# The first feed-forward product of a transformer block, with 20 of its 22 gated pairs as 7 block products in place of 8

## The chip, the cores and the metric

The kernel runs on one core of a Trainium2 chip. The metric is the time of one execution on the device in microseconds (us), as the median of several runs; lower is better. A core has five engines with a queue of instructions each: TensorE (PE, matrix products), VectorE (DVE), ScalarE (ACT), GpSimd (POOL) and SyncE (SP, which here issues loads). Each engine works through its own queue in order; semaphores make it wait for the others. Products accumulate in PSUM; all other data lies in SBUF, 128 partitions wide.

## The reference

One block over 512 latent tokens and 256 context tokens with 1024 features, in fp32. Its last part is what is changed here:

```
def _swiglu(u, w_in, w_out):
    a, b = jnp.split(u @ w_in, 2, axis=-1)
    return (jax.nn.silu(a) * b) @ w_out
...
        x = x + g2 * _swiglu(_modulate(_rms_norm(x, norm2_g[i]), sh2, sc2),
                             w_ffn_in[i], w_ffn_out[i])
```

`u` is 512 x 1024, `w_in` 1024 x 5632, `w_out` 2816 x 1024. The parts ahead (two token mixers and their projections) are the same in both kernels.

## The kernel before

Features lie on the partitions, tokens in the columns. An fp32 operand is split into a rounded part `hi` (type fp32r) and the rest `lo` (`split`, lines 217 to 219: a cast on ACT, a subtraction on DVE). A product of two such operands is three matmuls, `mm3`, lines 245 to 248: hi by hi, hi by lo, lo by hi.

The 2816 hidden features are 22 tiles of 128. Tile j needs a pair of weight tiles, one for `a` (through SiLU) and one for `b`. Each weight tile is 128x1024 (8 steps of 128 input features by 128 outputs) and comes by one load of 512 KB on SP into a ring of three buffers (`wraw`, NRAW = 3); its hi and lo parts lie in rings of four (`whi`, `wlo`). `blk` gives larger buffers from a common pool; a buffer there is free again when its last reader is done.

Pairs 0 and 1 are special: their weights (`wff`) are loaded early, and they are multiplied for the tokens 0 to 255 (A) and then 256 to 511 (B), in a section whose order is written out by hand (`tc.manual_schedule`, for PE, DVE and ACT). The norm of the tokens (`mod2`) is done there too, by the same halves, into `u2` (hi and lo for each of 8 feature tiles). For pairs 2 to 21, outside that section, a planner that lays the program out against its own estimate of the times sets the order of the instructions on each engine. A pair there is two `mm_tile` calls of 24 matmuls with 512 columns, each into a PSUM bank (`ps_f`), then `swiglu`: SiLU on ACT, a multiplication by the second tile on DVE, and the split of the result `h` into hi and lo. The next stage, `ffn_out`, multiplies the 22 h tiles by `w_out` (`wfo`), into `ps_fo`.

Of the kernel before, what the change touches and what calls it, by code (L numbers as in the profile page):

```python
# [56 lines left out]
# column map of the packed per-feature vectors  # L57
# [15 lines left out]
def block_kernel(ctx: ExitStack, tc: tile.TileContext, a, out):  # L73
# [90 lines left out]
    silc = cst.tile([P, NK, 4], F32, name="silc")  # silu(c), silu(c_ctx), 0, 0  # L164
# [9 lines left out]
    def rsqrt(v, n, nm):  # L174
        """v (fp32 [P, n]) -> 1/sqrt(v), Newton from an integer seed."""
# [10 lines left out]
    def sumsq_step(acc, ap, k, eng=vec):  # L186
        """acc += ap ** 2 (features on partitions)"""
        sq = tmp("sq")[:, :ap.shape[1]] if k else acc
        act.activation(sq, ap, AF.Square)
        if k:  # L190
            eng.tensor_tensor(acc, acc, sq, op=ALU.add)

    def part_sum(*parts):
        """-1/(2 D) * sum over the partitions, on every partition"""
        ps = psx("st")[:, :parts[0].shape[1]]
        for i, t in enumerate(parts):
            pe.matmul(ps, lhsT=halfd, rhs=t, start=i == 0, stop=i == len(parts) - 1)
        return ps
# [4 lines left out]
    def inv_newton(y, ps):  # L203
        """y = (1.5 + (ps - EPS / 2) * y * y) * y"""
# [5 lines left out]
    def inv_rms(ps):  # L210
        """1 / sqrt(mean square + EPS)"""
# [39 lines left out]
    s4 = cst.tile([P, NK, 2, 2], F32, name="s4")      # [feature tile, (shift, scale), (x, ctx)]  # L251
    # silu(c), silu(c_ctx) split: columns hi, hi, lo, lo
# [4 lines left out]
    bcs = blk("bcs")                  # 1/rms of the tokens: x 512, ctx 256  # L257
# [24 lines left out]
    st_ = {}                          # tiles passed between the steps  # L282
# [11 lines left out]
    def step(name):  # L294
        """one step of the startup; digits name feature tiles, groups of them and pieces of the weights"""
        op, d = name.rstrip("0123456789"), name[len(name.rstrip("0123456789")):]
        i = int(d) if d else 0
        if op == "warm":              # keeps the tensor engine's clock up until the products start
# [271 lines left out]
    def mlstm_rows():  # L570
# [203 lines left out]
    def mlstm_mix(h0, mv, mo):  # L774
        hs_ = (h0, h0 + 1)
        pm, qs = {}, {}
        for h in hs_:
# [6 lines left out]
            for d in range(2):  # L784
# [6 lines left out]
                # exponents of the kept part are at most 0; the rest is bounded and cut off  # L791
# [86 lines left out]
    def rowmaj(ap):                   # column-major [P, 512] viewed in row-major order  # L878
        return ap.rearrange("p (c r) -> p r c", r=ROWS)
# [17 lines left out]
    def to_feat(o_pairs, gate_, v0, nm):  # L897
        """normalised heads (token-major) * norm_g * gate -> feature-major hi/lo."""
# [25 lines left out]
    # u in column-major token order from here on  # L924
# [106 lines left out]
    hs = []  # L1031

    def h_alloc(j):
        if j < 16:
            t = blk(f"h{j}", F32R)
            return t[:, 0:512], t[:, 512:1024]
        if j < 20:
            return [bp.tile([P, EW], F32R, name=f"h{j}_{i}", tag="mid", bufs=8)[:, :512] for i in range(2)]
        return [tmp(f"h{j}_{i}", F32R)[:, :512] for i in range(2)]

    def swiglu(pa, pb, j, s):
        sl = tmp("sl")[:, s]
        act.activation(sl, pa, AF.Silu)
        vec.tensor_tensor(sl, sl, pb, op=ALU.mult)  # L1044
        split(hs[j][0][:, s], hs[j][1][:, s], sl)

    # norm 2 and the first FFN tiles by halves of the tokens; the second half's products cover the first half's norm
    u2 = []
# [16 lines left out]
    def mod2_t(k, s, bc):  # L1065
# [24 lines left out]
    def ff_k(pss, ts, k, s):  # L1090
        for ps, w in zip(pss, ts):
            mm3(ps[:, :256], w[0][:, k, :], w[1][:, k, :], u2[k][0][:, s], u2[k][1][:, s], k == 0, k == NK - 1)

    for k in range(NK):
        t = blk(f"u2_{k}", F32R)
        u2.append((t[:, 0:512], t[:, 512:1024]))
# [4 lines left out]
    with tc.manual_schedule(engines=MAN):  # L1101
# [4 lines left out]
        m = mod2(A, inv_rms(part_sum(accs[0], last)))  # L1106
# [187 lines left out]
```

## Time and profile before

| what | value |
|---|---|
| median of 3 runs | 1132.61 us (1132.25 to 1133.26) |
| span of the profiled execution (its own time is not given beside it) | 1130.2 us |
| busy in the span: PE, PE weight loads | 1093.2, 895.0 us |
| busy in the span: DVE, ACT, POOL | 582.5, 486.9, 132.3 us |
| loads of `wfi`, the weights of the changed product | 44 of 512 KB |

The page lists busy time by engine, the span in 40 slices with the clock that TensorE was granted, the chain of work that ended last, and groups of instructions. A row of a group names line, engine, operation, output <- inputs, shapes, count, then busy us, mean ns of one, and the engine's idle time just before, with who ended it. A row of the timeline begins with the start and the duration in us. A row of windows has the stretch, its length, the engine's busy time and instructions, the granted clock, the share of the DMA engines and GB/s. A row of waits has engine, line, what ended the wait, then total us, times, longest.

### The profile page before, as it was taken

The page shows a single profiled execution, that of the slowest core. Times are in us where ns is not written, and L with a number is a line of the kernel's source. Part 1 is how long each engine was busy: PE and PEld are TensorE (multiplying, and loading weights), DVE is VectorE, ACT ScalarE, POOL GpSimd, SP SyncE. Part 2 cuts the span into 40 slices and gives each one's busy share as a digit, 9 for nine tenths or more (in the row PEclk, how much of TensorE's full clock was granted, in tenths as well). Part 3 has the DMA queues.
Part 4 walks back from the last instruction along what each step waited for, and adds up shares of the span by engine and source line. Part 5 has one row for each costly group of instructions (what it writes and reads, how often), then busy time and mean ns, then how long its engine had stood idle before and what let it go on. Part 6 is the DMA issues. An engine that isn't in the chain of part 4 may idle for free.

```text
span 1130.2 us, 13311 instructions
## 1 busy us (share of the span) xinstructions
PE 1093.2 (97%) x5182; PEld 895.0 (79%) x5182; DVE 582.5 (52%) x1018; ACT 486.9 (43%) x779; POOL 132.3 (12%) x72
## 2 busy tenths in 40 slices
PE   5799999899999999999999999999999999999997
PEld 2378888688888888888888888898888888888886
DVE  5977785775275474694234444664333333323233
ACT  6569564452383265366563332454222222222121
POOL 4600100010000000049970000000000000000000
PEclk7799999999999999999999999999999999999998
DMA  9430311031031022148762223503222222232312
GB/s 344 177 107 1 113 38 45 1 112 39 0 113 38 19 91 78 56 171 290 253 224 105 93 93 119 216 1 112 93 93 94 93 94 93 89 101 86 103 52 75
DMA packets 34263, 116.29 MB, mean 103 GB/s; under 512 B 3960, under 2 KB 6264, under 8 KB 34200
## 3 DMA queue, kind: packets, MB, share of 16 engines
q1 hardware_dynamic: 32672, 114.25, 29.1%
q10 hardware_dynamic: 1528, 1.19, 0.3%
q8 instruction: 41, 0.67, 0.2%
q14 instruction: 22, 0.18, 0.0%
HBM read 113.33 MB, written 2.10 MB: 102 GB/s over the span
## 4 chain that ended last, share of the span: by engine, by line
PE 90%; DVE 4%; DMA 3%; ACT 2%; issue 0%; SPq 0%; DVEq 0%; ACTq 0%
PE ps_f L248 7%; PE ps_f L247 7%; PE ps_f L246 7%; PE ps_g L247 5%; PE ps_g L248 5%; PE ps_g L246 5%; PE ps_fo L248 4%; PE ps_fo L247 4%; PE ps_fo L246 4%; PE ps_v L432 3%; PE ps_v L433 3%; PE ps_v L434 3%; PE ps_br L246 3%; PE ps_br L248 3%; PE ps_br L247 3%; PE ps_mU L840 2%
## 5 line engine op out<-in xcount | busy, mean ns | idle before, releaser
L219 DVE TENSOR_TENSOR wlo<-wraw,whi 128x1024 fp32r<-128x1024 f32 x150 | 189.2, 1264 | 229.5 <-ACT whi L218 224.5
L218 ACT CAST whi<-wraw 128x1024 fp32r<-128x1024 f32 x150 | 155.0, 1037 | 348.4 <-issue 116.0
L248 PE MATMUL ps_f<-u,wlo 128*128 128x512 f32 x320 | 126.4, 395 | 0.0
L247 PE MATMUL ps_f<-u,whi 128*128 128x512 f32 x320 | 126.1, 394 | 0.0
L246 PE MATMUL ps_f<-u,whi 128*128 128x512 f32 x320 | 125.8, 393 | 0.0
L247 PE MATMUL ps_g<-ucm,whi 128*128 128x512 f32 x256 | 103.1, 403 | 0.0
L246 PE MATMUL ps_g<-ucm,whi 128*128 128x512 f32 x256 | 102.0, 399 | 0.0
L248 PE MATMUL ps_g<-ucm,wlo 128*128 128x512 f32 x256 | 102.0, 398 | 0.0
L968 POOL TENSOR_TENSOR wr<-wr,crow 128x1024 f32<-128x1024 f32 x32 | 89.5, 2835 | 66.1 <-ACT crow L961 65.9
L246 PE MATMUL ps_fo<-h,whi 128*128 128x512 f32 (+1 forms) x198 | 73.2, 370 | 0.0
L247 PE MATMUL ps_fo<-h,whi 128*128 128x512 f32 (+1 forms) x198 | 73.0, 369 | 0.0
L248 PE MATMUL ps_fo<-h,wlo 128*128 128x512 f32 (+1 forms) x198 | 73.0, 369 | 0.0
L247 PEld LDWEIGHTS ps_f<-u,whi 128*128 128x128 f32 x320 | 60.1, 188 | 14.4
L246 PEld LDWEIGHTS ps_f<-u,whi 128*128 128x128 f32 x320 | 60.1, 188 | 14.3
L248 PEld LDWEIGHTS ps_f<-u,wlo 128*128 128x128 f32 x320 | 60.0, 188 | 14.0
L246 PEld LDWEIGHTS ps_g<-ucm,whi 128*128 128x128 f32 x256 | 48.1, 188 | 11.2
L247 PEld LDWEIGHTS ps_g<-ucm,whi 128*128 128x128 f32 x256 | 48.1, 188 | 11.0
L248 PEld LDWEIGHTS ps_g<-ucm,wlo 128*128 128x128 f32 x256 | 48.1, 188 | 10.8
L1044 DVE TENSOR_TENSOR sl<-sl,ps_f 128x512 f32<-128x512 f32 (+1 forms) x24 | 15.4, 643 | 72.5 <-PE ps_f L248 71.4
L969 ACT ACTIVATE wr<-wr 128x1024 f32<-128x1024 f32 x32 | 33.9, 1060 | 35.5 <-POOL wr L968 35.5
L247 PEld LDWEIGHTS ps_fo<-h,whi 128*128 128x128 f32 x198 | 37.2, 188 | 6.9
L246 PEld LDWEIGHTS ps_fo<-h,whi 128*128 128x128 f32 x198 | 37.2, 188 | 6.8
(383 smaller groups left out, 2287.8 us busy)
## 6 DMA issues: line engine op xcount, KB each, us to landing
wraw<-in_wfi SPq DMA_DIRECT2D x44, 512.0 KB, 3.5
wraw<-in_wp SPq DMA_DIRECT2D x32, 512.0 KB, 3.5
wr<-in_wada_b SPq DMA_DIRECT2D x32, 512.0 KB, 4.3
wa<-in_wada_a SPq DMA_DIRECT2D x16, 512.0 KB, 10.1
wraw<-in_wfo SPq DMA_DIRECT2D x16, 512.0 KB, 3.4
wraw<-in_wgv SPq DMA_DIRECT2D x8, 512.0 KB, 3.5
wraw<-in_wmqk SPq DMA_DIRECT2D x8, 512.0 KB, 3.4
wraw<-in_wmv SPq DMA_DIRECT2D x8, 512.0 KB, 3.8
```

Source lines behind the costliest of these rows:

```text
L218: act.copy(hi, src)
L219: vec.tensor_tensor(lo, src, hi.bitcast(F32), op=ALU.subtract)
L246: pe.matmul(ps, lhsT=wh, rhs=xh, start=first, stop=False)
L247: pe.matmul(ps, lhsT=wh, rhs=xl, start=False, stop=False)
L248: pe.matmul(ps, lhsT=wl, rhs=xh, start=False, stop=last)
L432: pe.matmul(ps, lhsT=h_, rhs=wh, start=(k == 0), stop=False)
L433: pe.matmul(ps, lhsT=h_, rhs=wl, start=False, stop=False)
L434: pe.matmul(ps, lhsT=l_, rhs=wh, start=False, stop=(k == NK - 1))
L840: pe.matmul(ps[:, :257], lhsT=kw[(dh, c)], rhs=mv[c][:, h - h0, :], start=True, stop=True)
L968: pool.tensor_tensor(wr, wr, crow, op=ALU.mult)
L969: act.activation(wr, wr, AF.Identity, accum_out=ada[:, j:j + 1])
L1044: vec.tensor_tensor(sl, sl, pb, op=ALU.mult)
```

## The change

For pairs 2 to 21 the product of the 512 tokens with a pair's 1024 x 256 weights is seen as a product of 2 x 2 blocks: the tokens as A11, A12 (tokens A, features 0 to 511 and 512 to 1023), A21, A22 (tokens B); the weights as b11, b21 (the `a` tile's halves of the features) and b12, b22 (the `b` tile's). In Winograd's form of Strassen's scheme 7 block products take the place of 8, with sums of blocks ahead and behind:

- The token sums S1, S2, S3, S5 are built and split once (`s_blocks`: 4 sums and 4 subtractions on DVE, 4 casts on ACT, each 128x1024), in the section written by hand, beside the B-half products of pairs 0 and 1. For this `mod2` now keeps the fp32 tokens (`uf`).
- The weight sums are built for each pair (`wino_weights`): t1 and t3 on DVE, t2 and t4 on POOL, each 128x512; t2 needs t1, t4 needs t2. Split into hi and lo are g1 (the raw `a` tile), g2 (t2 and t1), g3 (t3 and t4), each 128x1024, and g4 (b22, 128x512).
- `prod` is a block product: 4 steps of 128 features by three matmuls with 256 columns, 12 in all, for 7 products 84 a pair. Before it was 48 of 512 columns. 960 matmuls of 512 columns go, 1680 of 256 come.
- Three PSUM banks X, Y, Z collect the products. X goes on accumulating after parts of it have been read: copies on ACT (p1, u2, q5, u3), sums on DVE (p1, cc[A]) and POOL (cc[B]), two SiLUs of 256 columns in place of one of 512, and the multiplication into `hf` (fp32).
- `h` is split into hi and lo after the loop of the pairs, in the program's next stage, every fourth subtraction on POOL.

```
@@ mod2: normed, modulated tokens, now kept in fp32 (uf) and as hi and lo blocks @@
-        t = tmp("ut")[:, :256]
-        vec.scalar_tensor_tensor(t, x1[k][:, s], a2c[:, k:k + 1], bc, op0=ALU.mult, op1=ALU.mult)
-        act.activation(u2[k][0][:, s], t, AF.Identity, bias=sh2c[:, k:k + 1])
...
+            vec.scalar_tensor_tensor(uf[i][:, c], x1[k][:, s], a2c[:, k:k + 1], bc, op0=ALU.mult, op1=ALU.mult)
+            act.activation(uf[i][:, c], uf[i][:, c], AF.Identity, bias=sh2c[:, k:k + 1])
...
+                vec.tensor_tensor(a_lo[i_][:, c_], uf[i_][:, c_], a_hi[i_][:, c_].bitcast(F32), op=ALU.subtract)
+            if k % 2:
...
+                act.copy(a_hi[i][:, c], uf[i][:, c])
...
+    def s_blocks():
...
+        a11, a12, a21, a22 = (u[:, :1024] for u in uf)
...
+        vec.tensor_tensor(a22, a21, a22, op=ALU.subtract)
+        g = hi_lo(1, a22)
...
+        vec.tensor_tensor(a21, a11, a21, op=ALU.subtract)
+        vec.tensor_tensor(a11, a22, a11, op=ALU.subtract)
...
+        vec.tensor_tensor(a12, a12, a11, op=ALU.add)
...
+    def prod(ps, w, o, x, first):
...
+        for k in range(4):
+            c, t = slice(o + k * P, o + k * P + P), slice(k * 256, k * 256 + 256)
+            for i, (y, z) in enumerate(((0, 0), (0, 1), (1, 0))):
+                pe.matmul(ps[:, :256], lhsT=w[y][:, c], rhs=x[z][:, t], start=first and k + i == 0,
+                          stop=k == 3 and i == 2, skip_group_check=not first)
...
+    def wino_weights(j):
+        raw = [flat(wload(a["wfi"][2 * j + i])[0]) for i in range(2)]
+        b11, b21 = raw[0][:, :512], raw[0][:, 512:]
+        b12, b22 = raw[1][:, :512], raw[1][:, 512:]
+        t21, t34 = blk("t21"), blk("t34")
+        t2, t1, t3, t4 = t21[:, :512], t21[:, 512:1024], t34[:, :512], t34[:, 512:1024]
...
+        vec.tensor_tensor(t1, b11, b12, op=ALU.add)
+        pool.tensor_tensor(t2, t1, b22, op=ALU.add)
+        g1 = pair(raw[0], "g1")
+        vec.tensor_tensor(t3, b12, b22, op=ALU.add)
+        pool.tensor_tensor(t4, t2, b21, op=ALU.add)
+        g2 = pair(t21[:, :1024], "g2")
+        g4 = blk("g4", F32R)
+        split(g4[:, :512], g4[:, 512:1024], b22)
+        g3 = pair(t34[:, :1024], "g3")
+        return g1, g2, g3, (g4[:, :512], g4[:, 512:1024])
...
     for j in range(2, NFF):
-        hs.append(h_alloc(j))
-        pab = []
-        for i in range(2):
-            w = wnext.pop(0) if wnext else wtile(a["wfi"][2 * j + i])
-            ps = psm("ps_f")
-            mm_tile(w, ps, u2)
-            pab.append(ps)
-        swiglu(pab[0], pab[1], j, slice(0, 512))
+        h_alloc(j)
+        g1, g2, g3, g4 = wino_weights(j)
+        X, Y, Z = psm("ps_X"), psm("ps_Y"), psx("ps_Z")
+        e1, e2, sl, cc = tmp("e1"), tmp("e2"), tmp("sl"), tmp("cc")
+        p1, u2, q5, u3 = e1[:, :256], e1[:, 256:512], e2[:, :256], e2[:, 256:512]
+        prod(X, g1, 0, A11, True)
+        act.copy(p1, X[:, :256])
+        prod(Y, g1, 512, A12, True)
+        vec.tensor_tensor(p1, Y[:, :256], p1, op=ALU.add)
+        act.activation(sl[:, A], p1, AF.Silu)
+        prod(X, g2, 0, sb[2], False)
+        act.copy(u2, X[:, :256])
+        prod(Z, g2, 512, sb[1], True)
+        act.copy(q5, Z[:, :256])
+        prod(X, g3, 0, sb[3], False)
+        act.copy(u3, X[:, :256])
+        pool.tensor_tensor(cc[:, B], q5, u3, op=ALU.subtract)
+        prod(Z, g4, 0, sb[5], False)
+        vec.tensor_tensor(cc[:, A], Z[:, :256], u2, op=ALU.subtract)
+        prod(X, g3, 512, A22, False)
+        act.activation(sl[:, B], X[:, :256], AF.Silu)
+        vec.tensor_tensor(hf[j], sl[:, :512], cc[:, :512], op=ALU.mult)
...
+    hs = []
+    for j in range(NFF):
+        t = blk(f"h{j}", F32R)
+        act.copy(t[:, :512], hf[j])
+        (pool if j % 4 == 3 else vec).tensor_tensor(t[:, 512:1024], hf[j], t[:, :512].bitcast(F32), op=ALU.subtract)
+        hs.append((t[:, :512], t[:, 512:1024]))
```

The order on each engine comes out of the planner, so the diff doesn't show it. In the rows below a name ends with the number of its buffer; X_6467 is X of pair 4, X_6593, g1h_6576, g2h_6582, g3h_6589, g4_6586, t21_6572 (t2 and t1) and t34_6573 are pair 5's, the numbers 6695 to 6716 are pair 6's.

PE before, from the second tile of pair 4 (ps_f_6363) to the first of pair 5 (ps_f_6400):

```order
L246 MATMUL ps_f_6363<-u2_7_5627,whi_6359 128x512
L247 MATMUL ps_f_6363<-u2_7_5627,whi_6359 128x512
L248 MATMUL ps_f_6363<-u2_7_5627,wlo_6360 128x512
L246 MATMUL ps_f_6400<-u2_0_5620,whi_6396 128x512
L247 MATMUL ps_f_6400<-u2_0_5620,whi_6396 128x512
L248 MATMUL ps_f_6400<-u2_0_5620,wlo_6397 128x512
```

PE now, from the last product of pair 4 (by A22, ah3 and al3) to the first products of pair 5 that read g2:

```order
L1180 MATMUL ps_X_6467<-ah3_6039,g3l_6464 128x256
L1180 MATMUL ps_X_6467<-ah3_6039,g3h_6463 128x256
L1180 MATMUL ps_X_6467<-al3_6040,g3h_6463 128x256
L1180 MATMUL ps_X_6467<-ah3_6039,g3l_6464 128x256
L1180 MATMUL ps_X_6593<-s2h_6067,g2h_6582 128x256
L1180 MATMUL ps_X_6593<-s2l_6068,g2h_6582 128x256
L1180 MATMUL ps_Z_6595<-s1h_6056,g2h_6582 128x256
L1180 MATMUL ps_Z_6595<-s1l_6057,g2h_6582 128x256
L1180 MATMUL ps_X_6593<-s2h_6067,g2l_6583 128x256
```

Two products of pair 5 (on g1) stand ahead of these rows now, so that the last product of pair 4 is followed by one on g2, the sum over POOL, where before the next tile read a plain cast of loaded weights.

ACT before, around the SiLU of pair 4 (sl_6388 is its output, whi_6396 to whi_6464 are weights of pairs 5 and 6):

```order
L218 CAST whi_6396<-wraw_6394 128x1024
L1043 ACTIVATE sl_6320<-ps_f_6270 128x512
L218 CAST whi_6427<-wraw_6425 128x1024
L218 CAST h3_6269<-sl_6320 128x512
L218 CAST whi_6464<-wraw_6462 128x1024
L1043 ACTIVATE sl_6388<-ps_f_6332 128x512
L218 CAST whi_6495<-wraw_6493 128x1024
```

ACT now, around the second SiLU of pair 4 (L1233):

```order
L1228 COPY e2_6471<-ps_X_6467 128x256
L1219 COPY e1_6596<-ps_X_6593 128x256
L1222 ACTIVATE sl_6598<-e1_6596 128x256
L1233 ACTIVATE sl_6472<-ps_X_6467 128x256
L218 CAST g4_6586<-wraw_6570 128x512
L218 CAST g2h_6582<-t21_6572 128x1024
L218 CAST g3h_6589<-t34_6573 128x1024
L218 CAST g1h_6703<-wraw_6695 128x1024
```

The SiLU of pair 4 had casts of weights of pairs 5 and 6 ahead of it; now the casts g4, g2h and g3h of pair 5 stand behind it.

DVE before, around the multiplication of pair 4 (L1044, sl_6388):

```order
L219 TENSOR_TENSOR wlo_6397<-wraw_6394,whi_6396 128x1024
L1044 TENSOR_TENSOR sl_6320<-sl_6320,ps_f_6295 128x512
L219 TENSOR_TENSOR wlo_6428<-wraw_6425,whi_6427 128x1024
L219 TENSOR_TENSOR h3_6269<-sl_6320,h3_6269 128x512
L219 TENSOR_TENSOR wlo_6465<-wraw_6462,whi_6464 128x1024
L1044 TENSOR_TENSOR sl_6388<-sl_6388,ps_f_6363 128x512
L219 TENSOR_TENSOR wlo_6496<-wraw_6493,whi_6495 128x1024
```

DVE now, around the multiplication of pair 4 (L1234; the buffer hf4 holds the results of pairs 4 and 5):

```order
L1221 TENSOR_TENSOR e1_6596<-ps_Y_6594,e1_6596 128x256
L1234 TENSOR_TENSOR hf4_6441<-sl_6472,cc_6473 128x512
L1201 TENSOR_TENSOR t21_6572<-wraw_6568,wraw_6570 128x512
L1204 TENSOR_TENSOR t34_6573<-wraw_6570 128x512
L219 TENSOR_TENSOR g4_6586<-wraw_6570,g4_6586 128x512
L219 TENSOR_TENSOR g2l_6583<-t21_6572,g2h_6582 128x1024
L219 TENSOR_TENSOR g3l_6590<-t34_6573,g3h_6589 128x1024
```

The subtractions for the weights of pair 5 stood ahead of the multiplication; now t1 and t3 of pair 5 (L1201, L1204) and what is built on them stand behind it.

POOL now, from t4 of pair 4 to t2 of pair 6 (L1229 is cc[B], here of pairs 3 and 4; before, POOL had no work in this stage):

```order
L1205 TENSOR_TENSOR t34_6447<-t21_6446,wraw_6442 128x512
L1229 TENSOR_TENSOR cc_6346<-e2_6344 128x256
L1229 TENSOR_TENSOR cc_6473<-e2_6471 128x256
L1202 TENSOR_TENSOR t21_6572<-t21_6572,wraw_6570 128x512
L1205 TENSOR_TENSOR t34_6573<-t21_6572,wraw_6568 128x512
L1202 TENSOR_TENSOR t21_6699<-t21_6699,wraw_6697 128x512
```

t2 and t4 of pair 5 follow the sum cc of pair 4, and pair 6 follows directly behind them.

More of the change, by code (lines that the diff above doesn't have):

```diff
@@ L1030, in block_kernel @@
     ww = [wtile(a["wo"][j]) for j in range(4, 8)]
-    hs = []
+    hf = []
     def h_alloc(j):
[L1034 to L1048, printed above, removed]
+        if j < 14:
+            if j % 2 == 0:
+                st_["hb"] = blk(f"hf{j}")
+            hf.append(st_["hb"][:, (j % 2) * 512:(j % 2) * 512 + 512])
+        else:
+            hf.append(mid(f"hf{j}")[:, :512])
     MAN = {mybir.EngineType.PE, mybir.EngineType.DVE, mybir.EngineType.Activation}
@@ L1088, in steps, with ff_k, hi_lo, swiglu_half @@
             next(g, None)
-    def ff_k(pss, ts, k, s):
+    def ff_k(pss, ts, k, h):
+        i, c = 2 * h + k // 4, slice((k % 4) * 256, (k % 4) * 256 + 256)
         for ps, w in zip(pss, ts):
[L1092 to L1096, printed above, removed]
+            mm3(ps[:, :256], w[0][:, k, :], w[1][:, k, :], a_hi[i][:, c], a_lo[i][:, c], k == 0, k == NK - 1)
+    def s_blocks():
+        a11, a12, a21, a22 = (u[:, :1024] for u in uf)
+        out = {}
+        def hi_lo(n, f):
+            out[n] = blk(f"s{n}h", F32R), blk(f"s{n}l", F32R)
+            act.copy(out[n][0][:, :1024], f)
+            yield
+            vec.tensor_tensor(out[n][1][:, :1024], f, out[n][0][:, :1024].bitcast(F32), op=ALU.subtract)
+            yield
+        vec.tensor_tensor(a22, a21, a22, op=ALU.subtract)
+        g = hi_lo(1, a22)
+        next(g)
+        vec.tensor_tensor(a21, a11, a21, op=ALU.subtract)
+        vec.tensor_tensor(a11, a22, a11, op=ALU.subtract)
+        yield out
+        g2 = hi_lo(2, a11)
+        next(g2)
+        next(g)
+        vec.tensor_tensor(a12, a12, a11, op=ALU.add)
+        g3 = hi_lo(3, a21)
+        next(g3)
+        next(g2)
+        yield
+        g5 = hi_lo(5, a12)
+        next(g5)
+        next(g3)
+        next(g5)
+        yield
+    def swiglu_half(pa, pb, j, s):
+        sl = tmp("sl")[:, s]
+        act.activation(sl, pa, AF.Silu)
+        vec.tensor_tensor(hf[j][:, s], sl, pb, op=ALU.mult)
     accs = [tmp(f"acc2{i}")[:, :256] for i in range(2)]
@@ L1105, in block_kernel @@
         ps = wo_half(4, B, accs[1], 0, W2A)
-        m = mod2(A, inv_rms(part_sum(accs[0], last)))
+        m = mod2(0, inv_rms(part_sum(accs[0], last)))
         steps(m, M2[0])
@@ L1117, in block_kernel @@
         for k in range(W2B):
-            ff_k(pss, wff, k, A)
-        m = mod2(B, inv_rms(part_sum(accs[1], last)))
+            ff_k(pss, wff, k, 0)
+        m = mod2(1, inv_rms(part_sum(accs[1], last)))
         act.activation(junk, ones[:, 0:1], AF.Silu)
         for k in range(W2B, NK):
-            ff_k(pss, wff, k, A)
+            ff_k(pss, wff, k, 0)
         drain(m)
-        hs += [h_alloc(0), h_alloc(1)]
+        h_alloc(0)
+        h_alloc(1)
+        m = s_blocks()
+        sb = next(m)
         for j in range(2):
-            swiglu(pss[2 * j][:, :256], pss[2 * j + 1][:, :256], j, A)
-        wnext = [wtile(a["wfi"][i]) for i in range(4, 8)]
+            swiglu_half(pss[2 * j][:, :256], pss[2 * j + 1][:, :256], j, A)
+        drain(m)
         for j, pf in enumerate((psx, psm)):
@@ L1130, in block_kernel @@
             for k in range(NK):
-                ff_k(pss, wff[2 * j:2 * j + 2], k, B)
-            swiglu(pss[0][:, :256], pss[1][:, :256], j, B)
-    for j in range(2, NFF):
-        hs.append(h_alloc(j))
-        pab = []
-        for i in range(2):
-            w = wnext.pop(0) if wnext else wtile(a["wfi"][2 * j + i])
-            ps = psm("ps_f")
-            mm_tile(w, ps, u2)
-            pab.append(ps)
-        swiglu(pab[0], pab[1], j, slice(0, 512))
+                ff_k(pss, wff[2 * j:2 * j + 2], k, 1)
@@ new lines, in block_kernel @@
+            swiglu_half(pss[0][:, :256], pss[1][:, :256], j, B)
+    def prod(ps, w, o, x, first):
[4 more added lines that the diff above has]
+                          stop=k == 3 and i == 2, skip_group_check=not first)
+    A11, A12, A22 = ((a_hi[i], a_lo[i]) for i in (0, 1, 3))
@@ new lines, in flat, with pair @@
+    def flat(t):
+        return t.rearrange("p k c -> p (k c)")
+    def wino_weights(j):
[4 more added lines that the diff above has]
+        t2, t1, t3, t4 = t21[:, :512], t21[:, 512:1024], t34[:, :512], t34[:, 512:1024]
+        def pair(f, nm):
+            hi = flat(wp.tile([P, NK, P], F32R, name=nm + "h", tag="whi", bufs=NHI))
+            lo = flat(wp.tile([P, NK, P], F32R, name=nm + "l", tag="wlo", bufs=NLO))
+            split(hi, lo, f)
+            return hi, lo
+        vec.tensor_tensor(t1, b11, b12, op=ALU.add)
[8 more added lines that the diff above has]
+        return g1, g2, g3, (g4[:, :512], g4[:, 512:1024])
```

27 lines of the change are left out of this document (15 added, 12 removed).

## Prediction

> **What bounds the kernel now.** I read the page first: the span, the busy shares, the slices and the chain that ended last.
>
> ```profile
> span 1130.2 us, 13311 instructions
> PE 1093.2 (97%) x5182; PEld 895.0 (79%) x5182; DVE 582.5 (52%) x1018; ACT 486.9 (43%) x779; POOL 132.3 (12%) x72
> ...
> PE   5799999899999999999999999999999999999997
> ...
> PEclk7799999999999999999999999999999999999998
> ...
> PE 90%; DVE 4%; DMA 3%; ACT 2%; issue 0%; SPq 0%; DVEq 0%; ACTq 0%
> ```
>
> The reader is to see that TensorE (PE) is the bound nearly everywhere: nine or more tenths of almost each slice, and 90% of the chain. The changed stage begins where pair 2 of the first feed-forward product begins and ends where `ps_fo` begins. The timeline of PE gives both places, and the start of the half-token products of pairs 0 and 1 (tokens B):
>
> ```profile
> 762.66 0.28 PE L246 MATMUL ps_f<-u,whb 128*128 128x256 f32 x1
> ...
> 774.03 0.39 PE L246 MATMUL ps_f<-u,whi 128*128 128x512 f32 x1
> ...
> 996.95 0.40 PE L246 MATMUL ps_fo<-h,whi 128*128 128x512 f32 x1
> ```
>
> Pairs 2 to 21 take 996.95 - 774.03 = 222.92 us for 20 x 48 = 960 matmuls of 512 columns, 232.2 ns each, 11.15 us for a pair. The 2 x 2 x 24 = 96 matmuls of 256 columns ahead take 774.03 - 762.66 = 11.37 us, 118.4 ns each. The list of PE's waits says that nothing is lost in the stage: its two largest entries at one place lie elsewhere, and no `ps_f` is among them.
>
> ```profile
> PE st L197 <- DVE CSQ L315: 6.2, 1, 6.2
> PE ps_s L681 <- ACT emq L649: 5.6, 1, 5.6
> ```
>
> So a matmul saved here is time saved, and any wait that the new work puts in front of PE is time lost.
>
> **Term 1, the matmuls.** A pair has 7 block products of 12 matmuls, 84 x 118.4 ns = 9.95 us, for 11.15 us before: 1.20 us less. Over 20 pairs: -24.0 us (1680 x 118.4 ns = 198.9 us for 222.9 us).
>
> **Term 2, the hand-over to each odd pair from 3 to 13.** The order of the changed kernel shows it for pair 5. PE does the first two products of pair 5 early; the last product of pair 4 (g3 by A22, into X) then stands directly ahead of the first matmul that reads `g2h` of pair 5. DVE has the multiplication `hf` of pair 4 ahead of the sums t1 and t3 of pair 5, and `hf` waits for ACT's second SiLU of pair 4, which waits for that same last product. t1 feeds POOL's t2, t2 feeds ACT's cast `g2h`, and this feeds DVE's `g2l`. Behind `hf` on DVE stand t1, t3, g4, `g2l`, `g3l`; behind the SiLU on ACT stand the casts of pairs 5 and 6. PE has nothing else in its queue, so the whole chain lies on its path. The same order stands at pairs 3, 7, 9, 11 and 13. The even pair after each is prepared in the same burst, while PE works on the odd one.
>
> The durations, by groups of the same shape: ACT and DVE in the stage, DVE while POOL is busy, POOL:
>
> ```profile
> L218 ACT CAST whi<-wraw 128x1024 fp32r<-128x1024 f32 x49 | 51.2, 1049 | 172.0 <-issue 84.8 <-PE ps_f L247 74.0 <-PE ps_wo L247 7.1
> L218 ACT CAST h<-sl 128x512 fp32r<-128x512 f32 x20 | 12.4, 622 | 0.3 <-DVE sl L1044 0.3
> L1043 ACT ACTIVATE sl<-ps_f 128x256 f32<-128x256 f32 x4 | 1.5, 379 | 0.0
> ...
> L219 DVE TENSOR_TENSOR wlo<-wraw,whi 128x1024 fp32r<-128x1024 f32 x51 | 62.3, 1224 | 82.0 <-ACT whi L218 79.1
> L1044 DVE TENSOR_TENSOR sl<-sl,ps_f 128x512 f32<-128x512 f32 x20 | 13.8, 688 | 71.4 <-PE ps_f L248 71.4
> L1044 DVE TENSOR_TENSOR sl<-sl,ps_f 128x256 f32<-128x256 f32 x4 | 1.7, 417 | 1.1 <-ACT sl L1043 1.1
> ...
> L219 DVE TENSOR_TENSOR wlo<-wraw,whi 128x1024 fp32r<-128x1024 f32 x18 | 29.2, 1627 | 54.7 <-ACT whi L218 54.7
> ...
> L342 POOL TENSOR_TENSOR alo<-wa,ahi x20: 1263/1466/1737, 9.1 to 54.7; 128x512 fp32r<-128x512 f32 x20
> L342 DVE TENSOR_TENSOR alo<-wa,ahi x12: 677/681/1765, 18.3 to 57.9; 128x512 fp32r<-128x512 f32 x12
> ```
>
> What lies between two engines is read from one stretch of the timeline:
>
> ```profile
> 796.08 0.40 PE L248 MATMUL ps_f<-u,wlo 128*128 128x512 f32 x1
> ...
> 796.32 1.05 ACT L218 CAST whi<-wraw 128x1024 fp32r<-128x1024 f32 x1 [4.03 <-issue]
> ...
> 796.58 0.69 DVE L1044 TENSOR_TENSOR sl<-sl,ps_f 128x512 f32<-128x512 f32 x1 [3.53 <-PE ps_f L248]
> ...
> 797.41 1.23 DVE L219 TENSOR_TENSOR wlo<-wraw,whi 128x1024 fp32r<-128x1024 f32 x1
> ```
>
> PE's modelled end 796.48 to DVE's start: 0.10 us. ACT's end 797.37 to DVE's start: 0.04 us. From the issue of the last matmul of a pair: its duration 0.28, hand-over 0.10, SiLU 0.38, 0.04, `hf` 0.69, t1 0.69, 0.04, t2 on POOL 1.47, 0.04, cast `g2h` 1.05, then 0.04, `g2l` 1.22, and 0.10 to PE: 6.14 us. Four matmuls that need `g2h` alone stand in the gap (0.47), and the next issue was due after 0.12. The stall is 6.14 - 0.47 - 0.12 = 5.55 us. t3, g4 (0.69 each on DVE) and t4 lie beside it: between t1's end and `g2l` DVE has 2.6 us for 1.4. The ends: with t2 at 1.26 and nothing slowed, 5.3; with t2 at 1.74 and `g2l` at the 1627 ns of the row beside a busy POOL (t4 runs then), 6.2.
>
> This also costs clock. The one wait of such a length in mid-kernel, by PE's timeline and by half microseconds with the granted clock in the fourth column:
>
> ```profile
> 220.54 0.40 PE L434 MATMUL ps_v<-whi,u 128*128 128x512 f32 x1
> 226.57 0.80 PE L681 MATMUL ps_s<-qd,E 128*128 128x128 f32 x2 [5.63 <-ACT emq L649]
> ...
> 222.50:223.00 0.50, 0.00 (x0) 0.91 0.00 0
> 223.00:223.50 0.50, 0.00 (x0) 0.50 0.00 0
> ...
> 229.50:230.00 0.50, 0.50 (x6) 0.76 0.42 90
> 230.00:230.50 0.50, 0.50 (x5) 1.00 0.62 197
> ```
>
> The clock halved about 2.0 us after PE fell idle (220.94 to about 222.95) and came back about 3.2 us after it began again (226.57 to about 229.75). In a hand-over PE idles some 4.6 us for `g2h`, does four matmuls, idles again, and goes on 6.1 us after the last issue. If the 3.2 us count from those four, at 4.9, some 2.0 us of work go at half the clock and lose 1.0 us; if from the resumption, 3.2 us lose 1.6. Ends 0 (no halving) and 1.6; I take 1.2. Six times 5.55 + 1.2 = 6.75 us: +40.5 us.
>
> The Trainium skill's "TensorE: Matmul & The Clock Gate", section "What's actually happening", has the clock halved after an idle window of about 3.4 us, in windows that run freely. The row agrees as far as it goes: halved at some point of a 5.6 us wait. By that rule a wait of 4.6 us holds a whole idle window in about a third of the phases ((4.6 - 3.4)/3.4, an estimate), which would take two thirds of 6 x 1.2 = 7.2 us from the sum: 1146.
>
> **Term 3, the start.** In mod2 16 subtractions of 256 columns become 8 of 512, and ACT gets 8 casts of 512 (0.62 each, 5.0 us over two halves, beside the `wo` and first `ps_f` products). The S blocks are 8 DVE operations of 128x1024 (8 x 1.22 = 9.8 us) and 4 ACT casts (4.2 us), beside the 11.37 us of B-half products: nothing on the path while those last, up to the 9.8 us without them. But t1 of pair 2 needs a block that the last B-half product frees: hand-over 0.38, t1 0.69, t2 1.47, cast 1.05, `g2l` 1.22, and 0.22 between = 5.03 us, against 24 matmuls on g1 (2.84) and 4 on `g2h` (0.47): +1.7 us (0 to 4).
>
> **Term 4, inside the stage.** A pair's sums by the rows: DVE 3 x 0.69 (t1, t3, `hf`) + 3 x 1.22 + 0.69 (splits) + 2 x 0.42 (PSUM) = 7.3 us; ACT 3 x 1.05 + 0.62 + five pieces of about 0.38 = 5.7; POOL 2 x 1.47 + about 0.75 = 3.7. All below 9.95, so from pair 14 on, where t1 of the next pair stands ahead, I count no stall (0 to 8 us over 8 pairs). PSUM copies that stand behind casts: +0.3 (0 to 4). Weight loads stay at 2 of 512 KB a pair on SP's queue, now freed by DVE's and POOL's readers:
>
> ```profile
> wraw<-in_wfi SPq DMA_DIRECT2D x44, 512.0 KB, 3.5
> ```
>
> t1, t2, t4, the load's 3.5 us and hand-overs close a loop of about 7.3 us, shorter than a pair.
>
> **Term 5, the split of h.** 20 casts (0.62) and 20 subtractions (0.69) leave the stage, and 22 of each stand in the next, 5 subtractions on POOL. The first `ps_fo` products take 3 x 232 = 0.70 us for each h tile, a cast 0.62, and the first tiles' splits stand ahead of pair 21's last products: 0 (0 to +3), covered by those products.
>
> **Sum** against the profiled execution: -24.0 + 40.5 + 1.7 + 0.3 = +18.5, span 1148.7 us. The runs' median of 1132.61 lies 2.4 above its span: 1151.1 us.
>
> **The rivals.** *Faster: no or few hand-over stalls.* The place is the same six; it needs the stall and its clock under (24.0 - 2.0)/6 = 3.7 us. Were t2 as fast as DVE's 0.69, the stall would still be 4.8; so it takes stalls at three pairs or fewer (-24.0 + 3 x 6.75 + 2.0 = -1.8). With none: 1132.6 - 24.0 + 2.0 = 1110.6. Against it: queues run in order, and `hf` needs the last product. For it: that PE may have work in hand there which I took as done.
>
> *Stalls, but the clock stays:* 1151.1 - 7.2 = 1143.9. For it: the four matmuls inside the gap; against it: halving after 2.0 us.
>
> *POOL and DVE shut each other out.* Then a pair costs DVE 7.3 + 3.7 = 11.0 us, 1.05 more than PE, and at the 8 pairs from 14 on DVE is the bound: +8.4, 1159.5, and t2 in the chain would wait for t3: 6 x 0.69 = 4.1 more, 1163.6. For it: DVE's 1765 ns beside POOL for 681 alone. Against it: while POOL was busy nearly all the time, DVE took 1627 for 1224, a third more, by which a pair's DVE work is 7.3 + 3.7 x 0.25 = 8.2 us, still under PE's. The Trainium skill's "GPSIMD Engine Reference", section "1. Specifications", says that POOL's SBUF interfaces are shared with VectorE, contended by instructions with two SBUF inputs, as t1, t3 and the splits are; this case's rows agree that there is a cost, and put it at a third.
>
> **How the numbers follow.** The forecast as summed, with its own spread of 1148 to 1158 from the stall's 5.3 to 6.2 and the clock's 1.0 to 1.6: 0.57. Clock stays: 0.17. POOL and DVE shut out, or other waits of that size in the stage: 0.13. Faster: 0.10. A net of nothing (four stalls of the smaller kind): 0.03. The range reaches from the clock rival with short stalls (1151.1 - 7.2 - 6 x 0.25 - 1.7 - 0.3 = 1140.4, less 4 for stalls missing at one pair) to the shut-out rival with 2 us for the start: 1136 to 1166. It leaves out the faster and level cases. A measurement of this kernel can't tell less than 0.2%, about 2.3 us, from no change: faster 0.10, same 0.03, slower 0.87.
>
> **What would show it.** Right: 118 ns from matmul to matmul inside a pair; in PE's waits an entry of six or twelve waits at `ps_X` for `g2h` on ACT and for `g2l` on DVE, 25 to 37 us together; the granted clock below 1.00 six times between 780 and 925 us, at intervals of about 27 us; none after pair 13; in the chain that ended last, POOL with some 9 us from t2. Wrong: no wait at `ps_X` before pair 14; the clock flat at 1.00; DVE as the releaser pair after pair at the end of the stage; `ps_fo` waiting for h.

## The result and the profile after

The changed kernel takes 1164.66 us (median of four runs, 1163.35 to 1165.76) for 1132.65 us before: ratio 1.0283, 95% interval 1.0268 to 1.0298. It is 32.0 us slower; the forecast was 1151, +18.5. The page of the profiled execution, the lines that answer to those shown of before:

```profile
span 1164.0 us, 15177 instructions
PE 1091.0 (94%) x5902; PEld 929.5 (80%) x5902; DVE 696.1 (60%) x1131; ACT 555.7 (48%) x929; POOL 225.9 (19%) x137
...
PE   5799999899999999999999999988888889999997
...
PEclk7799999899999999999999999998888889999998
...
PE 81%; DVE 7%; DMA 3%; ACT 3%; issue 3%; POOL 2%; SPq 0%; DVEq 0%; POOLq 0%; ACTq 0%
```

PE falls from 90% to 81% of the chain; DVE, ACT, POOL and time that the page calls issue (the engine waited for nothing that the profile shows) take its place there. The seven slices with 8 behind the middle of the span are pairs 2 to 13, and the granted clock dips in all of them but the first. PE's list of waits in the stage:

```profile
PE ps_X L1180 <- ACT g2h L218: 31.7, 7, 4.7
PE ps_X L1180 <- DVE g2l L219: 3.4, 7, 0.6
PE ps_Z L1180 <- ACT e L1226: 0.6, 1, 0.6
```

Seven waits for `g2h` and seven for `g2l`: pairs 2, 3, 5, 7, 9, 11 and 13, the six forecast and pair 2. None stands at the pairs from 14 on. One hand-over, from pair 4 to pair 5, in the rows of its chain out of the timeline of all engines (start, duration, engine; in brackets how long the engine had waited, and for whom):

```profile
824.16 0.28 PE L1180 MATMUL ps_X<-ah,g3l 128*128 128x256 f32 x1
824.48 0.38 ACT L1233 ACTIVATE sl<-ps_X 128x256 f32<-128x256 f32 x1 [0.41 <-PE ps_X L1180]
824.95 0.69 DVE L1234 TENSOR_TENSOR hf<-sl,cc 128x512 f32<-128x512 f32 x1 [1.40 <-ACT sl L1233]
825.56 0.69 DVE L1201 TENSOR_TENSOR t<-wraw 128x512 f32<-128x512 f32 x1
826.16 0.68 DVE L1204 TENSOR_TENSOR t<-wraw 128x512 f32<-128x512 f32 x1
826.38 1.59 POOL L1202 TENSOR_TENSOR t<-t,wraw 128x512 f32<-128x512 f32 x1 [4.95 <-issue]
826.76 1.75 DVE L219 TENSOR_TENSOR g<-wraw,g 128x512 fp32r<-128x512 f32 x1
828.00 1.05 ACT L218 CAST g2h<-t 128x1024 fp32r<-128x1024 f32 x1 [2.63 <-POOL t L1202]
828.04 1.59 POOL L1205 TENSOR_TENSOR t<-t,wraw 128x512 f32<-128x512 f32 x1
829.08 1.64 DVE L219 TENSOR_TENSOR g2l<-t,g2h 128x1024 fp32r<-128x1024 f32 x1 [0.57 <-ACT g2h L218]
829.10 0.58 PE L1180 MATMUL ps_X<-s2h,g2h 128*128 128x256 f32 x1 [4.66 <-ACT g2h L218]
830.77 0.58 PE L1180 MATMUL ps_X<-s2h,g2l 128*128 128x256 f32 x1 [0.46 <-DVE g2l L219]
```

Along the chain each step starts where the one ahead of it ends, to about 0.1 us: last product, SiLU, `hf`, t1, t2, cast, `g2l`. The rows L1204 (t3), `g` (g4's subtraction) and L1205 (t4) lie beside it. From the last issue to the first matmul with `g2l` are 6.61 us, in which five matmuls at 118.4 ns would have been due: 6.02 us lost. Then PE goes on at a granted clock of 0.50, and a matmul begins every 0.21 to 0.22 us in place of 0.118. The windows at which the clock falls and returns here (granted clock fourth):

```profile
826.40:826.60 0.20, 0.00 (x0) 0.89 0.00 0
826.60:826.80 0.20, 0.00 (x0) 0.50 0.00 0
833.20:833.40 0.20, 0.20 (x3) 0.55 0.30 123
833.40:833.60 0.20, 0.20 (x4) 1.00 0.25 102
```

It falls at 826.56 and returns at 833.38. From 830.77 to the first full-rate matmul at 833.46, 12 matmuls take 2.69 us in place of 1.42: 1.27 us more. The same reading at all seven places:

| place | last issue | first on g2h | first on g2l | full rate again | lost in the wait | lost to the clock behind it |
|---|---|---|---|---|---|---|
| pair 2 | 779.65 | 783.77 | 785.46 | 789.03 | 5.22 | 1.68 |
| pair 3 | 796.51 | 801.37 | 803.05 | 806.16 | 5.95 | 1.45 |
| pair 5 | 824.16 | 829.10 | 830.77 | 833.46 | 6.02 | 1.27 |
| pair 7 | 852.11 | 857.04 | 858.72 | 864.18 | 6.02 | 2.50 |
| pair 9 | 880.49 | 885.42 | 887.10 | 891.49 | 6.02 | 2.02 |
| pair 11 | 908.43 | 913.36 | 915.04 | 918.79 | 6.02 | 1.74 |
| pair 13 | 936.06 | 940.99 | 942.67 | 946.04 | 6.02 | 1.59 |

The sums are 41.3 and 12.2 us, 53.5 together. At pairs 2 and 3 the last issue is the last matmul of the pair's own products on g1, into Y.

### The profile page after: what moved, and what is told of

Its sections match the earlier page's. It is cut to its first block, busy times and chain, and to the rows that moved or that the text cites. A ratio compares the mean times of both kernels' runs of the same rounds, so it can differ in the third digit from the quotient of the medians.

```text
span 1164.0 us, 15177 instructions
## 1 busy us (share of the span) xinstructions
PE 1091.0 (94%) x5902; PEld 929.5 (80%) x5902; DVE 696.1 (60%) x1131; ACT 555.7 (48%) x929; POOL 225.9 (19%) x137
## 4 chain that ended last, share of the span: by engine, by line
PE 81%; DVE 7%; DMA 3%; ACT 3%; issue 3%; POOL 2%; SPq 0%; DVEq 0%; POOLq 0%; ACTq 0%
PE ps_X L1180 9%; PE ps_g L247 5%; PE ps_g L248 5%; PE ps_g L246 5%; PE ps_Z L1180 4%; PE ps_fo L248 4%; PE ps_fo L246 4%; PE ps_fo L247 4%; PE ps_v L432 3%; PE ps_v L433 3%; PE ps_v L434 3%; PE ps_br L246 3%; PE ps_br L248 3%; PE ps_br L247 3%; DMA wa<-in_wada_a 2%
## 5 line engine op out<-in xcount | busy, mean ns | idle before, releaser
L219 DVE TENSOR_TENSOR wlo<-wraw,whi 128x1024 fp32r<-128x1024 f32 (+1 forms) x110 | 140.4, 1278 | 138.7 <-ACT whi L218 136.4
L218 ACT CAST whi<-wraw 128x1024 fp32r<-128x1024 f32 (+1 forms) x110 | 113.2, 1033 | 180.4 <-PE ps_fo L247 69.7
L1202 POOL TENSOR_TENSOR t<-t,wraw 128x512 f32<-128x512 f32 x20 | 30.4, 1518 | 244.0 <-DVE t L1201 232.6
L1180 PE MATMUL ps_X<-s2h,g2h 128*128 128x256 f32 x80 | 27.3, 341 | 31.7 <-ACT g2h L218 31.7
L1180 PEld LDWEIGHTS ps_X<-s2h,g2h 128*128 128x128 f32 x80 | 18.6, 233 | 33.1 <-ACT g2h L218 33.1
L248 PEld LDWEIGHTS ps_fo<-h,wlo 128*128 128x128 f32 x198 | 37.2, 188 | 6.7
L686 POOL TENSOR_SCALAR_AFFINE_SELECT a<-a 128x512 f32<-128x512 f32 x8 | 7.8, 984 | 176.4 <-ACT a L683 175.9
L798 POOL TENSOR_SCALAR_AFFINE_SELECT pm<-pm 128x512 f32<-128x512 f32 x8 | 5.3, 668 | 186.3 <-ACT pm L795 186.3
L1229 POOL TENSOR_TENSOR cc<-e 128x256 f32<-128x256 f32 x20 | 18.4, 920 | 104.5 <-ACT e L1228 81.8
```

Of the source, the lines that this page charges most:

```text
L218: act.copy(hi, src)
L219: vec.tensor_tensor(lo, src, hi.bitcast(F32), op=ALU.subtract)
L248: pe.matmul(ps, lhsT=wl, rhs=xh, start=False, stop=last)
L1180: pe.matmul(ps[:, :256], lhsT=w[y][:, c], rhs=x[z][:, t], start=first and k + i == 0, stop=k == 3 and i == 2, skip_group_check=not first)
L1202: pool.tensor_tensor(t2, t1, b22, op=ALU.add)
```

## The experiments

**e1: no weight sums.** In `wino_weights`:

```
-        vec.tensor_tensor(t1, b11, b12, op=ALU.add)
-        pool.tensor_tensor(t2, t1, b22, op=ALU.add)
...
-        vec.tensor_tensor(t3, b12, b22, op=ALU.add)
-        pool.tensor_tensor(t4, t2, b21, op=ALU.add)
-        g2 = pair(t21[:, :1024], "g2")
+        g2 = pair(raw[0], "g2")
...
-        g3 = pair(t34[:, :1024], "g3")
+        g3 = pair(raw[1], "g3")
```

> The four weight sums of a pair (t1 to t4) are left out; g2 and g3 are split from the two raw tiles themselves, so the values are not the product's, but matmuls, splits, copies and loads are as many as in the changed kernel. Theory of the hand-over (g2 waits for a chain last product, SiLU, hf, t1, t2 on POOL, cast, at pairs 2, 3, 5, 7, 9, 11, 13; 41 us of waits and 12 us of halved clock): no chain, so 1164.7 - 53.5 = about 1111 us (1107 to 1116), no wait at ps_X over 1 us. Rival, the products themselves (reading X between its accumulations, banks that alternate, 256 columns) cost the time: most of the loss stays, 1138 us or more.

Measured: 1115.34 us, ratio to before 0.9844 (0.9830 to 0.9859). In its list of PE's waits nothing over 0.6 us is left from the changed stage on but one, in the next stage:

```profile
PE ps_fo L248 <- DVE wlo L219: 2.1, 1, 2.1
```

With the sums the waits are gone, and with them 49 us; 84 matmuls, a pair's number, take 9.91 to 10.07 us, so they and the PSUM copies cost what the rows of before gave. The time is 4 us above the 1111 expected, and that wait is 2.1 of it; the rest is not traced. The rival of costly products falls. What this run can't tell is whether the sums cost by their work or by their place.

**e2: the sums in another place.** The same work, with pairs 2 to 21 in an order written by hand for PE, DVE and ACT; the preparation of a pair is emitted in pieces during the pair before:

```
+    with tc.manual_schedule(engines=MAN):
+        prep(2, 2, 3, 4)
...
+            prep(j + 2, "loads")
+            prep(j + 1, "sums")
+            if late:
+                late()
             prod(X, d[1], 0, A11, True)
+            prep(j + 1, 1)
             act.copy(p1, X[:, :256])
...
             prod(X, d[2], 0, sb[2], False)
+            prep(j + 1, 2)
             act.copy(u2, X[:, :256])
...
             prod(X, d[3], 0, sb[3], False)
+            prep(j + 1, 3)
...
             vec.tensor_tensor(cc[:, A], Z[:, :256], u2, op=ALU.subtract)
+            prep(j + 1, 4)
             prod(X, d[3], 512, A22, False)
```

`prep(j + 1, n)` is the split of g1 to g4 of the next pair, "sums" its t1 to t4 (t2 and t4 on POOL as before), `late` the second SiLU and `hf` of the pair before, which now stand behind the sums.

> The same computation, the order of pairs 2 to 21 written by hand for PE, DVE and ACT: t1 and t3 of a pair stand ahead of hf of the pair before, g1 to g4 are split while the pair before is multiplied. Pair 2's own hand-over stays. Hand-over theory: six of seven places go, 6 x 7.75 = 46.5 us: 1118 us (1112 to 1125), one wait at ps_X for g2h, at pair 2. Rival, POOL and DVE in each other's way bound the stage wherever the sums stand: DVE or POOL become the releasers pair after pair, 1130 to 1150 us. Rival, the products cost it: 1155 us or more.

Measured: 1120.68 us, ratio 0.9891 (0.9877 to 0.9906). PE's waits in the stage:

```profile
PE ps_X L1180 <- ACT e L1240: 6.9, 1, 6.9
```

That one is pair 2's. From pair 3 on a pair begins every 9.94 to 9.98 us, 84 matmuls at 118.6 ns, with all sums on the same engines. So it was the place and not the load, and the rival of DVE and POOL as bounds of the stage falls too. Pair 2's wait came by another way than I expected: ACT's copy p1 stood behind splits that waited for POOL, and PE may not go on in X until it is copied.

**e3: the clock.** Idle matmuls in the wait:

```
+        if j in (2, 3, 5, 7, 9, 11, 13):
+            warm(32 if j == 2 else 38, st_["pe"] if j == 2 else st_["a22"])
         prod(X, g2, 0, sb[2], False)
```

> The changed kernel with 32 to 38 idle matmuls of 256 columns (product of a token block with itself into a spare PSUM bank, read by nobody) queued on PE in each of the seven places, behind the last product of the pair before, for 3.8 to 4.5 us of the wait. The chain is untouched. Hand-over theory with the clock as its second part: the waits stay as long, the granted clock stays at 1.00, and the 12.2 us after the waits and 2.3 us in the four matmuls inside them go: 1150 us (1147 to 1154). If the halved clock cost nothing, since PE then waits for other engines anyway: 1163 to 1166 us.

Measured: 1152.52 us, ratio 1.0174 (1.0159 to 1.0189). Windows at three of the places, then the wait left in PE's list:

```profile
820.00:830.00 10.00, 8.88 (x72) 1.00 0.33 107
846.00:856.00 10.00, 8.88 (x72) 1.00 0.31 105
872.00:882.00 10.00, 8.91 (x73) 1.00 0.30 107
```

```profile
PE ps_X L1180 <- DVE g2l L219: 6.2, 7, 1.0
```

The clock stays at 1.00 and 12.1 us go, for 14.5 expected: the four matmuls between the waits end sooner, but `g2l` comes no sooner, so its waits grow from 3.4 to 6.2 us, and the 2.3 us expected of those matmuls bring nothing. The halved clock behind the waits is a cost by itself: nearly all of the 12.2 us.

**e6: the chain made longer, e7: made otherwise.** First e6, then e7:

```
         pool.tensor_tensor(t2, t1, b22, op=ALU.add)
+        pool.tensor_tensor(t2, t1, b22, op=ALU.add)
```

```
-        pool.tensor_tensor(t2, t1, b22, op=ALU.add)
+        vec.tensor_tensor(t2, t1, b22, op=ALU.add)
...
-        pool.tensor_tensor(t4, t2, b21, op=ALU.add)
+        vec.tensor_tensor(t4, t2, b21, op=ALU.add)
```

> The changed kernel with t2 summed twice on POOL (the same operation again into the same place), for all 20 pairs. Hand-over theory: one more POOL operation of 1.59 us in the chain at seven places, nothing elsewhere: 1164.7 + 7 x 1.59 = 1175.8 us (1173 to 1179). Rival, POOL is a bound by its load: 20 x 1.59 = 31.8 us more, 1190 us or more. Rival, the chain is covered: 1165 us.

> The changed kernel with t2 and t4 on DVE, none on POOL. In this kernel's order on DVE t3 and g4's subtraction stand between t1 and t2, so t2 is ready after 4 x 0.61 us for 0.61 + 0.13 + 1.59 before: the same. What goes is POOL beside g2l, 1.22 for 1.64 us at seven places: 1164.7 - 2.9 = 1161.7 us (1159 to 1164). Rival, POOL's slow sum is the wait: t2 in 0.61 for 1.59 at seven places, 1157 us or less. Rival, DVE becomes the bound with 1.2 us more a pair: 1168 us or more, with DVE as the releaser at pairs 14 to 21.

Measured: e6 1175.14 us, ratio 1.0372 (1.0355 to 1.0389); e7 1160.68 us, ratio 1.0245 (1.0230 to 1.0261). PE's waits at `ps_X` in e6:

```profile
PE ps_X L1180 <- ACT g2h L218: 42.4, 7, 6.3
```

and in e7:

```profile
PE ps_X L1180 <- ACT g2h L218: 33.3, 7, 4.9
PE ps_X L1180 <- DVE g2l L219: 0.3, 1, 0.3
```

One operation of 1.59 us on POOL adds 10.5 us, about what seven of them come to (11.1), not twenty (31.8). By the traces, read as in the table above, the seven waits grow from 41.3 to 49.7 us and the loss to the clock from 12.2 to 12.9: the wait for `g2h` grows by 1.53 a place, but `g2l` gains some back, 1.31 us for 1.64 at pair 5, since t4 is nearly done when it starts. With both sums on DVE the wait for `g2h` is about as long as it was (33.3 for 31.7), since t2 then stands behind two other operations, and the wait for `g2l` all but goes, because no POOL operation runs beside it. POOL's slowness in itself was not the cause; the number of operations between the last product and `g2h` was.

**e4, e5, e8, e9: pair 2.** e4 is e2 with pair 2's sums in the gaps of the norm on DVE and its splits among those of the S blocks:

```
+        steps(m, 3)
+        prep(2, "sums")
         drain(m)
...
         next(g2)
+        prep(2, 2)
         next(g3)
+        prep(2, 3)
```

> e2 with pair 2's sums moved into the gaps of the norm's second half on DVE, and its splits placed among those of the S blocks. Hand-over theory: the seventh place goes too, or leaves under 1.5 us: 1111 us (1108 to 1116). Rival, DVE's S blocks bound the start whatever stands among them: 1116 to 1121 us, with a wait at ps_X for S2, S1 or g2 of pair 2.

Measured: 1120.75 us, ratio 0.9890 (0.9873 to 0.9906): no better than e2. The sums on DVE hold up the norm, on which PE waits (pair 2 begins at 778.84 for 776.78 in e2), and two copies still stand behind splits. The time is the rival's, but the waits are for copies, not for a block of S or g2. PE's waits:

```profile
PE ps_X L1141 <- ACT e L1249: 3.8, 1, 3.8
PE ps_X L1141 <- ACT e L1244: 1.2, 1, 1.2
PE ps_f L246 <- ACT ah L1079: 1.0, 1, 1.0
PE ps_f L247 <- DVE al L1076: 0.8, 2, 0.4
```

e5 has the four sums of pair 2 on POOL ahead of the section (`sums(2, pool)`), and in pair 2 the copies p1, u2 and u3 ahead of splits of pair 3; the first SiLU and the split of pair 3's g1 still stand ahead of the copy q5:

```
+            if j == 2:
+                prep(3, 1)
             prod(Z, d[2], 512, sb[1], True)
             act.copy(q5, Z[:, :256])
...
             act.copy(u3, X[:, :256])
+            if j == 2:
+                prep(3, 2, 3)
```

> The order of e2 with another start: pair 2's four sums all on POOL, ahead of the norm's section (POOL has no other work there), its splits among those of the S blocks; in pair 2 the PSUM copies stand ahead of the splits of pair 3 on ACT. In e2 and e4 PE still lost 7 and 5 us of waits plus the clock at pair 2, because the copies p1 and u2 stood behind splits that waited for POOL. Hand-over theory: no wait at ps_X over 1 us, clock 1.00 through pair 2, 1120.7 - 9 = 1112 us (1109 to 1115). Rival, DVE's S blocks bound the start: a wait of 2 us or more at pair 2 for a block of S or g2, 1115 to 1121 us.

Measured: 1115.24 us, ratio 0.9847 (0.9832 to 0.9862), just above what was expected and at the low end of the rival's range. The granted clock still fell once at pair 2, for 3.41 us. Its largest wait in the stage is for a copy, q5, not for a block of S or g2:

```profile
PE ps_Z L1141 <- ACT e L1255: 2.2, 1, 2.2
```

e8 moves the SiLU and the split of pair 3's g1 behind the copy q5; e9 is the same kernel once more.

```
-            if j == 2:
-                prep(3, 1)
             prod(Z, d[2], 512, sb[1], True)
             act.copy(q5, Z[:, :256])
+            if j == 2:
+                act.activation(sl[:, A], p1, AF.Silu)
+                prep(3, 1)
```

> e5 with one thing moved: in pair 2 the first SiLU, and the split of pair 3's g1 behind it, stand behind the copy q5 on ACT. In e5 q5 waited 2.2 us behind a SiLU that waited for DVE, and PE with it, with the clock halved after. Hand-over theory: no wait at pair 2 over 0.5 us: 1115.2 - 2.2 - 1.3 = 1112 us (1110 to 1114). Rival, DVE's S blocks bound the start, and the wait only moves to the next product that needs one (S5, g4 or g2 of pair 3): 1114 to 1117 us.

> The kernel of e8 once more, for a profile at full clock: that of e8 was taken while the granted clock was about 0.75 throughout. If q5's place was worth what the timeline of e5 says, no wait over 0.5 us stands at pair 2 and the difference to e5 lies elsewhere; if the wait only moved, one of 1 to 2 us stands at another product of pair 2 or 3. Time 1113 to 1116 us either way.

Measured: e8 1114.94 us, ratio 0.9842 (0.9829 to 0.9856); e9 1114.87, ratio 0.9840 (0.9824 to 0.9857). PE's waits in e9:

```profile
PE ps_X L1141 <- ACT e L1250: 1.1, 1, 1.1
PE ps_X L1141 <- ACT e L1261: 0.8, 1, 0.8
PE ps_Z L1141 <- ACT e L1254: 0.8, 1, 0.8
PE ps_X L1141 <- ACT e L1244: 0.4, 1, 0.4
```

Here the rival is right: the wait of 2.2 us has become four of 3.1 together, at pairs 2 and 3, all for copies on ACT. None of them lowers the granted clock, which stays at 1.00 through the stage. DVE's work on the S blocks stands ahead of what they wait for; that this is what bounds the start now is argued, no run isolates it. Still, e9 is 1.6% faster than the kernel before with the change's own products.

## Why the prediction was right, and where it was short

The sign and the mechanism held: 84 matmuls at 118 ns, a stall at six hand-overs, none from pair 14 on, and a clock that halves. The time lies at the upper end of the range, and outside the forecast's own spread of 1148 to 1158; the range held it only because it reaches to the price of a rival, and in that luck had a part. Between the two spans, 1130.2 and 1164.0, are 33.8 us:

| term | forecast | measured |
|---|---|---|
| 1: matmuls, 20 pairs | -24.0 | -23.8, by the 9.96 us a pair of e2 |
| 2: six hand-overs, the wait | 6 x 5.55 = 33.3 | 36.1 |
| 2: six hand-overs, the clock behind it | 6 x 1.2 = 7.2 | 10.5 |
| 3: norm, S blocks | 0 | +1.3 |
| 3: pair 2 | 1.7 | 6.9 |
| 4 and 5: inside the stage, splits of h | 0.3 | 1.2, the rest of the span |
| ahead of the changed code | - | +1.6 |
| sum | 18.5 | 33.8 |

- **The wait of a hand-over** was 6.02 us for 5.55. Step by step along the rows, `g2l` with its hand-over to PE took 1.69 for 1.32 (`g2l` itself 1.64 for 1.22, priced in the upper end) and t2 with its hand-over 1.62 for 1.51 (1.59 for 1.47); the others differ by under 0.1 each and cancel. `g2l` was held up by t4 and t2 by t3 (last section). The four matmuls at half clock lie beside `g2l` and cost nothing here. g4's subtraction, 1.75 beside t2, was hidden, as taken.
- **The clock** was the weaker half. I took 1.0 to 1.6 us from one wait; it was 1.27 to 2.50. The step that failed is the rule that the clock returns 3.2 us after PE begins again: here it returned 4.3 to 7.1 us after the first matmul on `g2h`, and 2.6 to 5.4 after the first on `g2l`. It went by a fixed grid of time (last section), so the length read at one wait did not carry over.
- **Pair 2** is the term that was mis-sized most. I set the S blocks against the whole 11.37 us of the B-half products. The timeline of DVE shows that they begin only when the norm's second half is done, 5.6 us after those products began, and t1 stands behind them:

```profile
769.84 1.23 DVE L1108 TENSOR_TENSOR uf<-uf,uf 128x1024 f32<-128x1024 f32 x1
...
779.09 1.22 DVE L1105 TENSOR_TENSOR s5l<-uf,s5h 128x1024 fp32r<-128x1024 f32 x1
780.23 0.68 DVE L1201 TENSOR_TENSOR t<-wraw 128x512 f32<-128x512 f32 x1
```

The last B-half product begins at 776.8; t1 starts 3.4 us after it, where I had 0.4. "Hidden beside" needs the start of the cover and of the covered, not only their lengths.
- **Ahead of the changed code** the same place (the first sum of squares in the section written by hand) lies at 739.29 before and 740.90 after, with the same source ahead of it; in e7's profile it lies at 739.33. It varies from profile to profile of kernels that are the same up to there (740.23 in e1, 739.68 in e6) and is not put down to the change.
- **The rivals.** No stalls (0.10) was refuted by the seven waits. That the clock stays (0.17) is refuted by the seven falls of the clock, and e3 shows that they cost time. That POOL and DVE shut each other out (0.13) gave the nearest time, 1159 to 1164. Its mechanism is what the trace shows (last section), and I was wrong to set it aside for a slowing by a third; but the price that I put on it is refuted. From pair 14 on nothing waits, and a pair's DVE work in the stage, by its groups and with its waiting for POOL, is 8.9 us (7.3 alone, 8.2 forecast, 11.0 by that rival), less than PE's 9.95; and t3 cost t2 some 0.3 us (1.59 for the 1.29 to 1.30 that it takes ahead of DVE's operations), not 0.69. A time alone would have spoken for that price; the places of the waits did not. The rule of the Trainium skill that was weighed ("TensorE: Matmul & The Clock Gate", section "What's actually happening") would have spared two thirds of the places; all seven lost clock, though only at pair 9 was PE idle through a whole window of the grid.

## What to carry to other kernels

Saving matmuls in a stage that PE fills pays only if what the new operands need is ready in time: follow, for each operand, the last thing its chain waits for, and see whether it is a product of the same PE queue directly ahead. Where a planner lays out the order from its own estimates, read that order at the places where one unit of work hands over to the next; here the same products and sums in another order, with pair 2's sums all on POOL, took 1114.9 us for 1164.7. Price a wait of PE with the clock that it loses, as a second term. Where a row has two lengths, as 681 and 1765 ns here, find out what ends the longer one before taking a mean.

## What the runs showed of the hardware

In these profiles the granted clock changes only at points of a fixed grid of 3.413 us. In the seven places it falls at 782.18, 799.25, 826.56, 857.28, 884.58, 911.89 and 939.19 and returns 6.82 or 6.83 us later each time; all of these are 0.53 or 0.54 us past a multiple of 3.4133. At pair 7 the windows are

```profile
857.20:857.40 0.20, 0.20 (x2) 0.69 0.00 0
...
864.00:864.20 0.20, 0.20 (x3) 0.75 0.00 0
```

There PE had stopped at 852.39 (852.11 and 0.28), and the clock fell only 4.9 us later, when PE was at work again, and then cost the most, 2.50 us; at pair 5 it fell 2.1 us after PE stopped (824.44), and cost the least. With the grid, the window that ends at 853.86 had PE idle for 1.5 of its 3.4 us and did not lower the clock; that of pair 5 (823.15 to 826.56) had 2.1 idle and did, and so did the one in the kernel before (idle 2.0). So a window need not be idle throughout. Between 740 and 1105 us, over the ten profiles read here, all 25 falls follow a window in which PE was at work for 41% or less, and no window with 53% or more brought one. The clock returned at the end of the first window that PE nearly filled: 87% or more of a window at work brought it back, 81% or less did not (one window of 88% in e6 did not either). So a fall lasted one window (3.41 us: once in e1 and e5, twice in e7), two, or, where PE began again late, three (10.24 us: three times in e6, once in e2). The Trainium skill ("TensorE: Matmul & The Clock Gate", "What's actually happening") tells of a free-running window of 3413 ns, and of a clock halved after an idle one: the runs agree on the window, and show that the fall needs less than a whole idle one.

DVE beside a POOL operation was not slowed by a third, as I took it from the adaLN stage: it waited until POOL's operation was done. In the hand-over shown, g4's subtraction took 1.75 us for 0.69 and ended (828.51) 0.54 us after t2 (827.97), and `g2l` took 1.64 for 1.22 and ended (830.72) 1.09 after t4 (829.63). It is so each time: of DVE's sums t1 and t3 and its splits of weights, 45 start in the stage while a POOL operation runs, and each ends 0.55 us (128x512) or 1.08 to 1.09 us (128x1024) after POOL's, 0.13 to 0.14 less than it takes alone. POOL waited for DVE likewise: t3 ends at 826.84 and t2 1.13 later, g4's subtraction at 828.51 and t4 1.12 later. DVE's sums with an operand in PSUM kept their 0.42 us beside POOL. The kernel before has it too: the longest of the L342 rows of the prediction, 1765 ns, is one of five of the twelve that start while POOL is at work, and all five end 0.55 us after POOL's operation; the mean of 1627 ns mixes such operations with others that were alone.
